# Nine of eleven feed-forward chunks by seven products, on weight pages grown in place by accumulating loads

## The chip, the core and the metric

The kernel runs on one core of one Trainium2 chip. The metric is device time in microseconds of one execution. The weights are float32 in HBM and are streamed through the chip in every execution.

## What is computed

One layer of a hybrid encoder on a sequence of 256 positions with 2048 channels. Two SwiGLU feed-forward layers (5632 hidden channels) stand around a mixer of mLSTM and attention:

```
def _swiglu(x, w1, w3, w2):
    return (jax.nn.silu(x @ w1) * (x @ w3)) @ w2

x   = _layer_norm(ALPHA * x + 0.5 * _swiglu(x, ffn1_w1[i], ffn1_w3[i], ffn1_w2[i]), ln1_g[i], ln1_b[i])
mix = _hybrid_mixer(x, ...)
x   = _layer_norm(ALPHA * x + mix, ln2_g[i], ln2_b[i])
x   = _layer_norm(ALPHA * x + 0.5 * _swiglu(x, ffn2_w1[i], ffn2_w3[i], ffn2_w2[i]), ln3_g[i], ln3_b[i])
x   = x + jax.nn.sigmoid(x @ w_ple_gate[i]) * (p[i] @ w_ple_proj[i])
```

The change touches the two feed-forward layers alone.

## The kernel before

**Matmuls in three parts.** TensorE works here on float32r operands. To keep precision each operand is split into a high part (a cast on ScalarE) and a low part (a subtraction on VectorE), and a product is high x high + high x low + low x high. Weights come as pages: a page is 256 rows by 512 columns of a weight (512 KB, tile `raw`, 128 partitions x 1024 values). `split_one` makes of it two pages `split`: ScalarE's cast at L972, VectorE's subtraction at L976. A *unit* is one page against one half of the sequence (128 positions): six matmuls of 512 columns, lines L1021 to L1023, into a bank `mm` of PSUM. In plain code (`group`) one split page serves two units, one for each half of the sequence.

**Chunks.** The 5632 hidden channels are worked in eleven chunks of 512 columns. A plain chunk has 16 units for the gate (w1), 16 for the hidden part (w3), then evictions, transposes (L247) and the down projection (w2), 16 units a chunk.

**Seven products.** Gate and hidden columns of both halves of the sequence together are a 2 x 2 block product: the activations' halves of the sequence by two halves of the channels, the weights' two halves of the channels by w1 and w3. `seven` does it with seven products instead of eight (numbered m = 1 to 7), four units each, 28 units for a chunk instead of 32. Three products take a page of the weights as it is (b11, b21 of w1, b12, b22 of w3), the others sums: b11 + b12, b11 + b12 + b22, b12 + b22, and the last one plus b21. They also need sums of activations (`forms`), made once for a layer by `form_turn`. Each side page is split for one unit only, where a plain page serves two. Before the change 7 of 11 chunks go this way.

Before, the page b11 + b12 is made at load time: SP loads b12 (L945) and POOL adds b11 to it with an accumulating load (L949, `accum_op=ALU.add`). The other sums are made by VectorE on pages (L308), or, in every second step, by one more accumulating load. The seven results are kept in seven banks, and VectorE adds them up (L404, L413, L452).

**Order.** The order is written out by hand. TensorE, VectorE, ScalarE, POOL and SP each work their instructions off in the order in which the program recorded them. `program` is the list of units in TensorE's order: plain units (`main`), with the side units of the seven-product chunks woven between them evenly (`weave`). `splits_due` records splits ahead of TensorE, up to SPLIT_FFN = 7 split weights at a time; `loads` records loads ahead of the splits, up to RAW_FFN pages. All pages come from one pool of 44 (PAGES). Short pieces of work (evictions, transposes) are recorded by `Sched` when they fall due by a clock that counts TensorE's units; its delays set only the order. Banks of PSUM: eight, in one rotating pool.

## Time and profile before

| what | value |
|---|---|
| time, median of 3 runs | 2230.02 us (2229.87 to 2230.93) |
| span of the profiled execution | 2228.3 us |
| mean granted TensorE clock | 0.998 |
| TensorE, VectorE, ScalarE busy | 99%, 76%, 54% of the span |
| HBM read | 533.56 MB, 240 GB/s over the span |
| plain loads of feed-forward weights (SP) | 639 of 512 KB, median 6.2 us to landing |
| accumulating loads (POOL) | 84 of 512 KB, median 9.0 us to landing |

The first feed-forward layer takes about the first 700 us of the span, the mixer the next 700, the second feed-forward layer about 1430 to 2110 us. In a window's row the columns are the window and its length, then for PE, PEld, DVE, ACT and POOL the busy us and in brackets the number of instructions, then the granted clock, the DMA engines' mean share, and GB/s. In a group's row stand the line, engine and operation, what is written from what, the count, busy us and the mean ns of one, and the idle time before them with what ended it. A busy matmul row is longer than its step to the next, since matmuls are pipelined; the step is read from a timeline.

### The profile page before, as it was taken

Reading aid. Unit: us, or ns where it says so; the run is one execution under the profiler, and the core shown is the slowest. Engines: PE = TensorE matmul, PEld = TensorE weight load, DVE = VectorE, ACT = ScalarE, POOL = GpSimd, SP = SyncE. Lnnn points to the kernel's source line nnn. Section 1 sums busy time; section 2 is a strip of 40 time slices with the busy share of each in tenths; the row PEclk is TensorE's granted clock in tenths of the full one; section 3 lists DMA queues with packets and bytes.
Section 4 is the critical chain, followed back from the end, with each engine's and each line's share of the span. In section 5 each row is a group of like instructions: output and inputs, shape, how many; then the busy total and the mean of one; then the engine's idle time right before and its main releaser. Section 6 shows DMA issues by size and latency. Waiting matters only on the chain.

```text
span 2228.3 us, 27828 instructions
## 1 busy us (share of the span) xinstructions
PE 2209.5 (99%) x10107; PEld 1832.6 (82%) x10107; DVE 1703.1 (76%) x1878; ACT 1197.9 (54%) x1383; POOL 152.3 (7%) x131
## 2 busy tenths in 40 slices
PE   9999999999999999999999999999999999999999
PEld 7888888888887888888888888788888888888878
DVE  6999888989888674654445466798888898989873
ACT  6655655555562655545643354465555555556452
POOL 2100100001000000101100000200100100100000
PEclk9999999999999999999999999999999999999999
DMA  9998999899993755555455566589999989999543
GB/s 333 280 293 278 277 290 305 273 290 288 288 319 97 225 182 169 185 166 169 153 191 193 183 228 216 187 242 295 273 282 289 286 276 299 283 294 321 201 159 96
DMA packets 281354, 537.50 MB, mean 241 GB/s; under 512 B 16832, under 2 KB 25856, under 8 KB 281216
## 3 DMA queue, kind: packets, MB, share of 16 engines
q1 hardware_dynamic: 258368, 491.68, 65.4%
q0 software_dynamic: 22848, 44.05, 11.4%
q8 instruction: 79, 1.29, 0.2%
q14 instruction: 59, 0.48, 0.1%
HBM read 533.56 MB, written 2.10 MB: 240 GB/s over the span
## 4 chain that ended last, share of the span: by engine, by line
PE 96%; DVE 3%; issue 0%; ACT 0%; DMA 0%; DVEq 0%
PE mm L1023 31%; PE mm L1021 31%; PE mm L1022 31%; PE ms L247 1%; DVE xres L368 1%; DVE xres L366 0%; DVE xres L369 0%; DVE stats L353 0%; DVE actT L254 0%; DVE split L976 0%; PE ms L741 0%; PE ms L764 0%; PE ms L692 0%; PE ms L704 0%; PE ms L754 0%
## 5 line engine op out<-in xcount | busy, mean ns | idle before, releaser
L976 DVE TENSOR_TENSOR split<-raw,split 128x1024 fp32r<-128x1024 f32 (+1 forms) x989 | 1162.3, 1206 | 314.5 <-ACT split L972 276.8
L972 ACT CAST split<-raw 128x1024 fp32r<-128x1024 f32 (+1 forms) x989 | 994.8, 1039 | 522.9 <-PE mm L1023 222.0
L1021 PE MATMUL mm<-split,actT 128*128 128x512 f32 (+2 forms) x3168 | 1233.9, 389 | 0.0
L1023 PE MATMUL mm<-split,actT 128*128 128x512 f32 (+2 forms) x3168 | 1223.4, 386 | 8.6 <-DVE actT L254 8.6
L1022 PE MATMUL mm<-split,actT 128*128 128x512 f32 (+2 forms) x3168 | 1221.8, 386 | 0.3 <-DVE split L976 0.3
L1023 PEld LDWEIGHTS mm<-split,actT 128*128 128x128 f32 x3168 | 596.4, 188 | 131.4 <-DVE actT L254 11.6
L1022 PEld LDWEIGHTS mm<-split,actT 128*128 128x128 f32 x3168 | 596.9, 188 | 116.4 <-DVE split L976 0.8
L1021 PEld LDWEIGHTS mm<-split,actT 128*128 128x128 f32 x3168 | 596.9, 188 | 116.3 <-issue 1.0
L949 POOL DMA_DIRECT2D raw<-in_ffn_w_dram x84 | 101.2, 1205 | 1087.4 <-DMA raw<-in_ffn_w_dram 371.6
L308 DVE TENSOR_TENSOR raw<-raw 128x1024 f32<-128x1024 f32 x140 | 170.9, 1221 | 1.0
L249 ACT CAST actT<-ms 128x512 fp32r<-128x512 f32 x84 | 49.1, 589 | 132.6 <-PE ms L247 122.5
L466 DVE SCALAR_TENSOR_TENSOR xres<-mm,xres 128x512 f32<-128x512 f32 x128 | 87.3, 686 | 12.7 <-PE mm L1023 12.5
L413 DVE TENSOR_TENSOR temp<-mm,temp 128x512 f32<-128x512 f32 x98 | 67.4, 687 | 13.1 <-PE mm L1023 11.5
L254 DVE TENSOR_TENSOR actT<-ms,actT 128x512 fp32r<-128x512 f32 x84 | 57.3, 686 | 22.7 <-ACT big L253 11.2
L383 POOL TENSOR_SCALAR xres<-xres 128x512 f32<-128x512 f32 x16 | 26.7, 1675 | 331.5 <-DVE xres L366 300.5
L219 ACT ACTIVATE temp<-mm 128x512 f32<-128x512 f32 (+1 forms) x26 | 14.7, 567 | 53.1 <-PE mm L1023 53.1
L219 ACT ACTIVATE temp<-temp 128x512 f32<-128x512 f32 (+1 forms) x44 | 26.0, 590 | 29.7 <-DVE temp L756 21.9
L219 ACT ACTIVATE big<-mm 128x512 f32<-128x512 f32 x20 | 12.0, 599 | 55.4 <-PE mm L1023 55.4
L215 ACT ACT_TABLE_LOAD x29 | 37.2, 1283 | 0.5
L811 DVE TENSOR_TENSOR big<-mm,big 128x512 f32<-128x512 f32 x16 | 11.1, 692 | 30.0 <-PE mm L1023 30.0
L897 DVE TENSOR_TENSOR temp<-temp,big 128x512 f32<-128x512 f32 (+1 forms) x10 | 5.8, 585 | 36.4 <-ACT temp L219 36.4
L219 ACT ACTIVATE rstd<-mv,eps 128x1 f32<-128x1 f32 x6 | 1.8, 296 | 51.8 <-DVE mv L359 51.8
(113 smaller groups left out, 513.7 us busy)
## 6 DMA issues: line engine op xcount, KB each, us to landing
raw<-in_ffn_w_dram SPq DMA_DIRECT2D x639, 512.0 KB, 6.2
raw<-in_w_in_dram SPq DMA_DIRECT2D x168, 512.0 KB, 3.7
raw<-in_ffn_w_dram POOLq DMA_DIRECT2D x84, 512.0 KB, 9.0
raw<-in_w_out_dram SPq DMA_DIRECT2D x32, 512.0 KB, 4.5
raw<-in_w_ple_gate_dram SPq DMA_DIRECT2D x24, 512.0 KB, 4.9
raw<-in_w_up_m_dram SPq DMA_DIRECT2D x16, 512.0 KB, 3.6
raw<-in_w_up_sb_dram SPq DMA_DIRECT2D x16, 512.0 KB, 4.1
raw<-in_w_ple_gate_dram SPq DMA_DIRECT2D x16, 256.0 KB, 5.2
```

The source lines that it names most:

```text
L219: nc.scalar.activation(out, in_, func, **kw)
L249: nc.scalar.copy(dst[:, 0], ps[:])
L254: nc.vector.tensor_tensor(out=dst[:, 1], in0=ps[:], in1=dst[:, 0], op=ALU.subtract)
L308: nc.vector.tensor_tensor(out=out.tile[:, :, :cols], in0=a.tile[:, :, :cols], in1=b.tile[:, :, :cols], op=ALU.add)
L413: nc.vector.tensor_tensor(out=out, in0=a, in1=b, op=op)
L466: nc.vector.scalar_tensor_tensor(out=xs, in0=ps, scalar=0.5, in1=xs, op0=ALU.mult, op1=ALU.add)
L949: nc.gpsimd.dma_start(out=r.tile[:, :, :r.cols], in_=r.plus, accum_op=ALU.add)
L972: nc.scalar.copy(hi[:, ks], r[:, ks])
L976: nc.vector.tensor_tensor(out=lo[:, ks], in0=r[:, ks], in1=hi[:, ks], op=ALU.subtract)
L1021: nc.tensor.matmul(ps, hi, w[0][:, k, :u.cols], start=first, stop=False)
L1022: nc.tensor.matmul(ps, hi, w[1][:, k, :u.cols], start=False, stop=False)
L1023: nc.tensor.matmul(ps, lo, w[0][:, k, :u.cols], start=False, stop=last)
```

## The change

Nine of eleven chunks go by seven products; chunks 0 and 5 stay plain. `seven` now loads b11 into a page, splits it for product 1, lets POOL add b12 to the same page, splits it for product 5, lets POOL add b22, splits it for product 6, lets VectorE add b21, and splits it for product 4. All of 1 (four units), then all of 5, two empty places in the weave, all of 6, then 2 and 4 in turn, then 7 and 3 in turn. b12 + b22 is always made by VectorE. Results are summed in PSUM: products 1 and 2 in one bank (X), 5 and 4 in one (E), 6 and 3 in one (B), 7 in one (W). B and W are two banks set aside; VectorE writes X - E into B before product 6, ScalarE copies B into W after it, and matmuls accumulate on top. Eight matmuls of ones at the start, in place of five, set these banks up for that. Six banks rotate instead of eight. Up to 12 raw pages may be loaded, if a count of pages in use lets them.

```diff
-RAW_FFN, RAW_MIX, RAW_EDGE = 9, 5, 4
+RAW_FFN, RAW_MIX, RAW_EDGE = 12, 5, 4
-PSUM_BUFS = 8
+PSUM_BUFS = 6
...
+    seeded = [seed_pool.tile([P, COL], F32, name=f"seeded{k}") for k in range(2)]
...
     def seven(wa, wb, rows, col0, cols, act, done):
         n = rows // (4 * P)
-        accs = {m: {} for m in range(1, 8)}
+        banks = {k: {} for k in "XEBW"}
...
+        def grow(raw, src):
+            def load():
+                nc.gpsimd.dma_start(out=raw.tile[:, :, :cols], in_=src.src, accum_op=ALU.add)
+            return load
...
-        units = []
-        for m, sub in ((1, 0), (2, 2)):
-            for i in range(n):
-                units.append(unit(m, i, plain(rows_of(wa, (4 * i + sub) * P, col0, cols)), act, 0, sub))
         for i in range(n):
-            b11, b12, b22, b21 = (rows_of(w, (4 * i + sub) * P, col0, cols)
-                                  for w, sub in ((wa, 0), (wb, 0), (wb, 2), (wa, 2)))
-            t1 = Raw(b12.src, cols, b11.src)
-            t3, add = (Raw(b12.src, cols, b22.src), None) if i % 2 else (b12, plus(b12, b12, b22))
-            first = Weight(t1, [t1], [])
-            units += [
-                unit(5, i, first, act.forms, 0, 0),
-                unit(7, i, Weight(t3, [t3, b22], [t3], add), act.forms, 1, 0),
-                unit(6, i, Weight(t1, [], [], plus(t1, t1, b22), first), act.forms, 0, 2),
-                unit(4, i, Weight(b21, [b21], [t1, b21], plus(b21, t1, b21)), act, 1, 2),
-                unit(3, i, Weight(b22, [], [b22]), act.forms, 1, 2),
-            ]
-        return units
+            t, b21 = quarter(wa, i, 0), quarter(wa, i, 2)
+            w1, w5, w6 = Weight(t, [t], []), Weight(t, [], []), Weight(t, [], [])
+            w1.then, w5.then = grow(t, quarter(wb, i, 0)), grow(t, quarter(wb, i, 2))
+            one.append(unit(1, i, w1, act, 0, 0, "X", True))
+            five.append(unit(5, i, w5, act.forms, 0, 0, "E", True))
+            six.append(unit(6, i, w6, act.forms, 0, 2, "B", False))
+            two.append(unit(2, i, Weight(b21, [b21], []), act, 0, 2, "X", False))
+            four.append(unit(4, i, Weight(t, [], [t, b21], plus(t, b21)), act, 1, 2, "E", False))
+            b12, b22 = quarter(wb, i, 0), quarter(wb, i, 2)
+            rest.append(unit(7, i, Weight(b12, [b12, b22], [b12], plus(b12, b22)), act.forms, 1, 0, "W", False))
+            rest.append(unit(3, i, Weight(b22, [], [b22]), act.forms, 1, 2, "B", False))
+        lead = two[:1]
+        for i in range(n):
+            lead += two[i + 1:i + 2] + four[i:i + 1]
+        return one + five + [None, None] + six + lead + rest
...
+            def done(m, banks):
+                ps = {k: v["ps"][:] for k, v in banks.items() if v}
+                if m == 5:
+                    e = temp()
+                    nc.scalar.copy(e[:], ps["E"])
+                    banks["B"]["ps"], banks["W"]["ps"] = seeded
+                    both(banks["B"]["ps"][:], ps["X"], e[:], ALU.subtract)
+                    drop()
+                elif m == 6:
+                    nc.scalar.copy(banks["W"]["ps"][:], ps["B"])
...
-        gate, hidden = zip(*(up(c) for c in (0, 3, 6, 9)))
+        gate, hidden = zip(*(up(c) for c in (0, 5)))
...
-        main = flat(hidden[0] + gate[1] + down(0) + hidden[1] + down(1) + gate[2] + down(2, 3)
-                    + hidden[2] + down(4) + gate[3] + down(5, 6) + hidden[3] + down(7) + rest[:8])
-        program.extend(main[:8] + weave(main[8:], [u for c in (1, 2, 4, 5, 7, 8, 10) for u in up7(c)]))
+        main = flat(hidden[0] + gate[1] + down(0) + down(1) + down(2) + down(3) + down(4) + hidden[1] + down(6) + down(5, 7))
+        program.extend(main[:8] + weave(main[8:] + flat(rest[:8]), [u for c in (1, 2, 3, 4, 6, 7, 8, 9, 10) for u in up7(c)]))
...
-    warm(WARM)
+    for ps in seeded:
+        for k in range(4):
+            nc.tensor.matmul(ps[:, k * P:(k + 1) * P], ones[:], ones[:], start=k == 0, stop=k == 3)
...
-        while pos["load"] < most and pos["raw"] < (4 if pos["at"] < 6 else limits(pos["split"])[0]):
+        while (pos["load"] < most and pos["raw"] < (4 if pos["at"] < 6 else limits(pos["split"])[0])
+               and (mixing() or pages[0] + pos["raw"] + 2 * limits(pos["split"])[1] < PAGES)):
...
+        if w.then:
+            w.then()
```

Where the instructions stand. POOL's queue before, for the second seven-product chunk of the first layer (each row is one accumulating load, named by the page it adds to; the page was loaded by SP ahead of it):

```order
L949 DMA raw_1211<-in_ffn1_w1_dram 128x2x512
L949 DMA raw_1325<-in_ffn1_w1_dram 128x2x512
L949 DMA raw_1372<-in_ffn1_w3_dram 128x2x512
L949 DMA raw_1478<-in_ffn1_w1_dram 128x2x512
L949 DMA raw_1598<-in_ffn1_w1_dram 128x2x512
L949 DMA raw_1618<-in_ffn1_w3_dram 128x2x512
```

Each page is added to once. The same queue now, for the third chunk by seven products:

```order
L328 DMA raw_1414<-in_ffn1_w3_dram 128x2x512
L328 DMA raw_1427<-in_ffn1_w3_dram 128x2x512
L328 DMA raw_1460<-in_ffn1_w3_dram 128x2x512
L328 DMA raw_1474<-in_ffn1_w3_dram 128x2x512
L328 DMA raw_1414<-in_ffn1_w3_dram 128x2x512
L328 DMA raw_1427<-in_ffn1_w3_dram 128x2x512
L328 DMA raw_1460<-in_ffn1_w3_dram 128x2x512
L328 DMA raw_1474<-in_ffn1_w3_dram 128x2x512
```

Eight instead of six a chunk, four pages twice each, and each stands behind a split that reads the page.

ScalarE's queue before, in the first such chunk, around a page that an accumulating load made (raw_875, then the same page with more added; the rows between are plain pages):

```order
L972 CAST split_1023<-raw_875 128x1024
L972 CAST split_1034<-raw_888 128x1024
L972 CAST split_1047<-raw_918 128x1024
L972 CAST split_1066<-raw_875 128x1024
L972 CAST split_1078<-raw_960 128x1024
```

The page is split for product 5 and again, after VectorE has added b22 to it, for product 6. ScalarE's queue now, in the third chunk, from the last cast for product 5 to the copy of bank E (mm_1722 is E):

```order
L995 CAST split_1685<-raw_1474 128x1024
L995 CAST split_1696<-raw_1501 128x1024
L266 CAST actT_1714<-ms_1709 128x512
L995 CAST split_1718<-raw_1414 128x1024
L995 CAST split_1729<-raw_1520 128x1024
L995 CAST split_1746<-raw_1427 128x1024
L995 CAST split_1756<-raw_1460 128x1024
L995 CAST split_1767<-raw_1474 128x1024
L443 COPY temp_1777<-mm_1722 128x512
```

The copy stands behind the casts of all four pages for product 6. VectorE's queue at the same place, to the seed of bank B (seeded0; mm_1635 is X):

```order
L999 TENSOR_TENSOR split_1719<-raw_1414,split_1718 128x1024
L999 TENSOR_TENSOR split_1730<-raw_1520,split_1729 128x1024
L999 TENSOR_TENSOR split_1747<-raw_1427,split_1746 128x1024
L999 TENSOR_TENSOR split_1757<-raw_1460,split_1756 128x1024
L999 TENSOR_TENSOR split_1768<-raw_1474,split_1767 128x1024
L437 TENSOR_TENSOR seeded0_78<-mm_1635,temp_1777 128x512
```

The seed stands behind the four splits for product 6; before the change no matmul waited for an eviction of its own chunk.

More of the change, by code (lines that the diff above doesn't have):

```diff
@@ L134, in __init__ @@
         self.start, self.stop, self.done = start, stop, done
+        self.onto = False
         tile.uses += 1
+        act.planned(chunk, tt)
 class Boundary:
@@ L153, in weave @@
             while at < len(side) and at * n < seen * len(side):
-                out.append(side[at])
+                if side[at] is not None:
+                    out.append(side[at])
                 at += 1
@@ L300, in seven, with unit @@
         n = rows // (4 * P)
-        accs = {m: {} for m in range(1, 8)}
-        def unit(m, i, tile, src, half, sub):
-            return Unit(tile, half, accs[m], src, i, sub, i == 0, i == n - 1, lambda ps, t, m=m: done(m, ps))
-        def plus(out, a, b):
+        banks = {k: {} for k in "XEBW"}
+        def unit(m, i, tile, src, half, sub, bank, first):
+            u = Unit(tile, half, banks[bank], src, i, sub, first and i == 0, i == n - 1,
+                     lambda ps, t, m=m: done(m, banks))
+            u.onto = not first
+            return u
@@ L1027 @@
             splits.pop(j)
+        if u.act.used(u.chunk, u.tt):
+            pages[0] -= 1
         if u.stop:
```

90 lines of the change are left out of this document (46 added, 44 removed).

## The prediction

> **What bounds the kernel now.** I read the page's first and fourth parts, the busy time of a long stretch inside the first feed-forward layer, and the list of waits there, in that order. A window's columns are: length; PE, PEld, DVE, ACT, POOL busy (instructions); granted clock; DMA share; GB/s.
>
> ```profile
> PE 2209.5 (99%) x10107; PEld 1832.6 (82%) x10107; DVE 1703.1 (76%) x1878; ACT 1197.9 (54%) x1383; POOL 152.3 (7%) x131
> PE 96%; DVE 3%; issue 0%; ACT 0%; DMA 0%; DVEq 0%
> 60.00:640.00 580.00, 580.00 (x2599) 480.47 (x2598) 517.52 (x513) 336.91 (x351) 49.30 (x41) 1.00 0.94 287
> ACT split L972 <- DMA raw<-in_ffn_w_dram: 8.8, 6, 2.4
> ```
>
> The chain that ended last is 96% TensorE, and in the feed-forward stretch TensorE never idles at full clock. But VectorE is busy 517.52 / 580 = 89% there and the DMA engines 94%. So matmuls taken out are gained only as long as the two nearly full resources deliver on time. Now they do: ScalarE waited 8.8 us in 580 for a weight page.
>
> What a matmul costs, and what a stall of TensorE does besides its own length, stands around the first layer norm:
>
> ```profile
> 704.15 0.39 PE L1023 MATMUL mm<-split,actT 128*128 128x512 f32 x1
> ...
> 704.83 0.39 PE L1023 MATMUL mm<-split,actT 128*128 128x512 f32 x1
> ...
> 706.06 0.40 PE L1022 MATMUL mm<-split,actT 128*128 128x512 f32 x1
> 709.16 0.50 PE L1023 MATMUL mm<-split,actT 128*128 128x512 f32 x1 [2.71 <-DVE actT L254]
> ...
> 710.78 0.63 PE L1022 MATMUL mm<-split,actT 128*128 128x512 f32 x1
> 711.21 0.63 PE L1023 MATMUL mm<-split,actT 128*128 128x512 f32 x1
> 710.00:720.00 10.00, 9.59 (x42) 7.55 (x41) 9.33 (x17) 1.96 (x4) 0.00 (x0) 0.83 0.09 27
> ```
>
> Three steps in 0.68 us: a matmul takes 0.227 us, a unit of six 1.36 us. After 2.71 us of idling the step is 0.43 us for a while and the granted clock of the next 10 us is 0.83, so 1.7 us more are lost.
>
> The accumulating loads, which the change leans on, are priced by these rows (queue q0 is POOL's, q1 is SP's):
>
> ```profile
> q1 hardware_dynamic: 258368, 491.68, 65.4%
> q0 software_dynamic: 22848, 44.05, 11.4%
> raw<-in_ffn_w_dram SPq DMA_DIRECT2D x639, 512.0 KB, 6.2
> raw<-in_ffn_w_dram POOLq DMA_DIRECT2D x84, 512.0 KB, 9.0
> DMA to landing us min/median/max: 5.7/9.0/12.8
> ```
>
> q0: 11.4% of 2228.3 us is 254 us on each of the 16 engines, 3.02 us for each of 84 loads. q1: 65.4% is 1457 us for 491.68 MB, or 938 loads of 512 KB: 1.55 us each. An accumulating load thus holds all 16 engines twice as long as a plain one. The quickest landed after 5.7 us, so about 2.7 us are fixed.
>
> **The change part by part.** Prices of one instruction:
>
> ```profile
> L976 DVE TENSOR_TENSOR split<-raw,split 128x1024 fp32r<-128x1024 f32 x955 | 1139.7, 1224 | 299.3 <-ACT split L972 263.9 <-PE mm L1022 16.8 <-issue 5.4
> L972 ACT CAST split<-raw 128x1024 fp32r<-128x1024 f32 x955 | 975.7, 1054 | 516.4 <-PE mm L1023 222.0 <-PE mm L1022 181.6 <-DVE raw L308 38.5
> L308 DVE TENSOR_TENSOR raw<-raw 128x1024 f32<-128x1024 f32 x140 | 170.9, 1221 | 1.0
> L413 DVE TENSOR_TENSOR temp<-mm,temp 128x512 f32<-128x512 f32 x98 | 67.4, 687 | 13.1 <-PE mm L1023 11.5
> L419 ACT COPY temp<-mm 128x512 f32<-128x512 f32 x14 | 8.3, 590 | 30.4 <-PE mm L1023 30.4
> ```
>
> *Two more chunks by seven products.* A chunk of 32 units becomes one of 28. Two chunks in each of two layers: 4 x 4 x 6 = 96 matmuls less, 96 x 0.227 = **-21.8 us**, all on TensorE, which is the path.
>
> *VectorE.* Per layer the splits go from 16 x 4 + 28 x 7 + 88 = 348 to 16 x 2 + 28 x 9 + 88 = 372, +24 x 1.22 = +29.4 us; page sums from 70 to 72, +2.4 us; evictions of up-projections from 9 x 7 + 2 x 4 = 71 to 4 x 9 + 2 x 2 = 40, -31 x 0.69 = -21.3 us. Net +10.5 us on some 0.89 x 650 = 580 us, over 640 us: 92%. It stays below TensorE, so I cost it at nothing; its cover is the 8% that are left. ScalarE gains 24 casts (25 us) and two copies a chunk, from 58% to about 63%: hidden.
>
> *DMA volume.* Plain loads per layer fall from 320 to 264, accumulating ones rise from 42 to 72: 320 x 1.55 + 42 x 3.02 = 623 us against 264 x 1.55 + 72 x 3.02 = 627 us. The mean load is unchanged. What changes is when it comes.
>
> *Accumulating loads move from the prefetch into the chunk.* This is the term that decides. Before, such a load was issued with the prefetch, several splits ahead of its use. Now the page is split for product 1, b12 is added, it is split for product 5, b22 is added, and it is split for product 6. POOL issues four, then four again, and the second four stand behind splits that wait for the first four. Then comes the seed: bank B = X - E. ScalarE's copy of E and VectorE's subtraction stand behind the casts and splits for product 6 on their in-order queues, behind all four of them in 8 chunks of 18, behind three in 10. And the first matmul of product 6 accumulates onto bank B, so TensorE, in order, stands still with all woven plain work behind it until seven or eight accumulating loads have landed.
>
> What that needs, worked out from the rows: one split (1.05 + 1.22 = 2.3 us), the fixed 2.7 us, eight times 3.02 = 24.2 us of all 16 engines, then a cast, a split and the seed, 1.05 + 1.22 + 0.69 = 3.0 us (the copy, 0.59 us, lies beside the split). That is 32.2 us, or 29.2 us where seven suffice. What covers it is TensorE's work between the matmul whose end lets the first split run and product 6. Counted from the program's semaphores: in the sixteen regular chunks 119 to 134 matmuls with their transposes, on average 28.8 us at 0.227 us each; in the first chunk of layer 1 31.3 us, in that of layer 2 37 us. So the need is above the cover even if no plain load shares the engines, by 3.4 and 0.4 us.
>
> Plain loads do share them. In this stretch side pages are held, not freed, so only woven plain weights let new loads through: 28.8 us hold 21 units, 184 of 436 of them plain, about 9 units or 4.5 loads. I take four, 6.2 us. The waits are then 9.6 us (eight chunks) and 6.6 us (eight), 4.1 us in layer 1's first and none in layer 2's first: 76.8 + 52.8 + 4.1 = **+133.7 us**. The bounds: without plain loads 8 x 3.4 + 8 x 0.4 = 30 us. At most I let a load take 5.05 us, from the longest landing, (12.8 - 2.7) / 2, if that one had stood behind another: 8 + 8 x 5.05 = 48.4 and 43.4 us, waits of 19.6 and 14.6 us, 273.6 us. I take the value nearest the mean packet time of q0, since q0 will be the fuller queue there.
>
> *The clock.* Seventeen waits longer than the 2.71 us above, at 1.7 us each: **+28.9 us**. Nothing at least, if the cases above are the short ones.
>
> *Small edits, together.* The seeded banks are set up by eight matmuls of ones instead of five:
>
> ```profile
> 1.12 2.50 PE L914 MATMUL ms<-ones 128*128 128x128 f32 x10 [1.12 <-DVE eps L228]
> 4.34 0.87 PE L247 MATMUL ms<-ident,xres 128*128 128x128 f32 x3 [0.72 <-DMA xres<-in_x_dram]
> ```
>
> Sixteen records of 0.25 us end at 5.1 us, not 3.6, where x lets TensorE go on at 4.34: +0.8 us. Six rotating banks instead of eight: X and E hold two, the plain pair two, two are free; the old scheme held up to five of eight for a chunk, so nothing. Deeper raw limit with a page count: nothing to a few us, inside the plain loads' term.
>
> *Sum.* 2228.3 - 21.8 + 0.8 + 133.7 + 28.9 = 2369.9 us. The profiled span is 1.7 us below the median of the runs shown, 2230.02 us, so I predict **2372 us**.
>
> A rule that speaks for the opposite, on its own: the Trainium skill, DMA: Bandwidth & Descriptors, section on the anatomy of one DMA on the SWDGE path, gives a fixed 2.0 us plus bytes / 436 GB/s. By it 512 KB move in 1.2 us (an estimate from that page), eight in 9.6 us, and the chain would be hidden. The rows show 3.02 us for this accumulating form, so I do not follow it.
>
> **The rivals.**
> *The growth is hidden (faster).* It decides at 8.0 + 8 x s = 28.8 us, s = 2.6 us per accumulating load, with plain loads yielding. Then only the removed matmuls count: 2230.0 - 21.8 + 0.8 = 2209 us. For it: 3.02 us includes sharing. Against it: no sum of rows reaches 2.6, and plain loads come on top.
> *Growth alone counts (slightly slower).* Plain loads run before or after it: 30 us of waits, half of them (8 x 1.7) with a lowered clock: 2230.0 - 21.8 + 0.8 + 30.4 + 13.6 = 2253 us.
> *Growth at 5.05 us a load (much slower).* 2230.0 - 21.8 + 0.8 + 273.6 + 12.1 + 28.9 = 2524 us, with 43.4 - 31.3 = 12.1 us for layer 1's first chunk. The median landing of 9.0 us speaks for crowding, the lower plain traffic in the stretch against it.
> *DMA volume is the bound.* The share is 94% now and the volume is unchanged: the old pace holds and the time stays at 2230 us. Against it: ScalarE waits 8.8 us in all for DMA now.
>
> **How the numbers follow.** Forecast 0.57 (its own range 2300 to 2440 us), hidden 0.12, growth alone 0.15, 5.05 us a load 0.12, volume 0.04. The low end of the range, 2240 us, leaves out the hidden and the volume case; the high end, 2490 us, takes in most of what lies between the forecast and the third rival. No change can be told within 0.2%, 4.5 us: faster 0.12, same 0.04, slower 0.84.
>
> **What would show it.** Right: TensorE's share falls to about 93%, and the largest wait of TensorE is that of the first seeded matmul for VectorE's seed (L437), some 16 times 6 to 10 us. ScalarE's split waits for DMA in the hundreds of us. POOL's loads land after a median above 12 us. The granted clock falls below 1.0 seventeen times more. VectorE's share does not rise above 90% of the layer. Wrong: no such wait, accumulating loads landing in 6 to 9 us though issued four in a row. The weakest step is the cover of 28.8 us: were VectorE to run the first split earlier, or the four plain loads be gone by then, each microsecond a chunk is 18 us in the sum.

## The result, and the profile after

The kernel after takes 2355.45 us (median of 4 runs, 2350.49 to 2361.89) against 2230.11 us before (4 runs, 2229.87 to 2230.93): a ratio of 1.0565, with a 95% interval of 1.0546 to 1.0584. It is slower by 125 us. The profiled execution took 2361.89 us with a span of 2360.2 us, 6 us above the median.

The page of the kernel after, its first, third and last parts (busy time; DMA queues with packets, MB and share of 16 engines' span; DMA issues with KB each and median us to landing):

```profile
PE 2236.6 (95%) x10017; PEld 1839.7 (78%) x10017; DVE 1734.9 (74%) x1884; ACT 1260.3 (53%) x1471; POOL 221.4 (9%) x191
...
q1 hardware_dynamic: 227904, 432.95, 55.8%
q0 software_dynamic: 39168, 75.51, 18.0%
...
raw<-in_ffn_w_dram SPq DMA_DIRECT2D x527, 512.0 KB, 6.2
...
raw<-in_ffn_w_dram POOLq DMA_DIRECT2D x144, 512.0 KB, 9.6
```

There are 90 matmul records fewer (96 taken out, six more in the set-up), and yet TensorE's busy time rose and its share fell. The same long stretch of the first layer, with the columns of the prediction's window:

```profile
60.00:640.00 580.00, 536.38 (x2318) 438.17 (x2317) 489.41 (x479) 335.61 (x362) 69.42 (x58) 0.96 0.84 237
```

TensorE issues 2318 matmuls in these 580 us where it issued 2599, at a granted clock of 0.96 instead of 1.00. VectorE is less busy than before (489 against 518 us) and the DMA engines too (0.84 against 0.94). So nothing is full any more; something waits. What TensorE waited for (us in total, times, longest), and after it ScalarE's largest wait:

```profile
PE seeded L1046 <- DVE seeded L437: 84.2, 16, 8.9
PE mm L1046 <- ACT actT L258: 12.8, 4, 6.7
PE mm L1048 <- DVE actT L272: 7.5, 6, 2.7
PE mm L1047 <- DVE split L999: 4.7, 8, 0.8
...
ACT split L995 <- DMA raw<-in_ffn_w_dram: 250.2, 132, 7.3
```

The first line is new: in 16 of 18 chunks the first matmul of product 6 waits 5.3 us on average for VectorE's seed of bank B. All lines of TensorE's waits come to 118.3 us, 13.8 us before. One such wait in order of time, in the fifth chunk: POOL's accumulating loads, ScalarE, VectorE and TensorE (start, length, then what the engine idled for just before).

```profile
348.50 1.20 POOL L328 DMA_DIRECT2D raw<-in_ffn_w_dram  x1 [50.16 <-DVE split L999]
...
369.33 1.20 POOL L328 DMA_DIRECT2D raw<-in_ffn_w_dram  x1 [2.35 <-DVE split L999]
```

```profile
373.74 1.05 ACT L995 CAST split<-raw 128x1024 fp32r<-128x1024 f32 x1 [2.54 <-DMA raw<-in_ffn_w_dram]
376.26 1.99 ACT L995 CAST split<-raw 128x1024 fp32r<-128x1024 f32 x2 [1.48 <-DMA raw<-in_ffn_w_dram]
378.16 0.58 ACT L443 COPY temp<-mm 128x512 f32<-128x512 f32 x1
```

```profile
377.34 2.36 DVE L999 TENSOR_TENSOR split<-raw,split 128x1024 fp32r<-128x1024 f32 x2 [1.29 <-ACT split L995]
379.62 0.68 DVE L483 SCALAR_TENSOR_TENSOR xres<-mm,xres 128x512 f32<-128x512 f32 x1
380.22 0.69 DVE L437 TENSOR_TENSOR seeded<-mm,temp 128x512 f32<-128x512 f32 x1
```

```profile
374.48 0.40 PE L1048 MATMUL mm<-split,actT 128*128 128x512 f32 x1
380.96 0.80 PE L1046 MATMUL seeded<-split,actT 128*128 128x512 f32 x1 [6.09 <-DVE seeded L437]
381.56 0.63 PE L1047 MATMUL seeded<-split,actT 128*128 128x512 f32 x1
381.99 0.63 PE L1048 MATMUL seeded<-split,actT 128*128 128x512 f32 x1
```

Eight loads are issued from 348.5 to 369.3. The casts start as their pages land, 2.5 to 3.7 us apart. TensorE had finished product 5 and all plain work ahead of product 6 at 374.7, but ScalarE's copy of E (L443) runs only behind three of the casts for product 6, at 378.2, and the seed behind VectorE's splits, at 380.2. The fourth cast stands behind the copy, so this seed needed seven of the eight loads. When TensorE goes on at 380.96 its steps are 0.43 us instead of 0.227. The granted clock around this wait, by windows (the column behind the engines' busy times):

```profile
371.40:374.80 3.40, 3.40 (x18) 2.55 (x16) 1.09 (x1) 1.05 (x1) 0.00 (x0) 1.00 1.13 225
374.80:378.40 3.60, 0.08 (x1) 0.00 (x0) 2.29 (x2) 2.13 (x3) 0.00 (x0) 1.00 1.10 242
378.40:381.00 2.60, 0.04 (x1) 0.04 (x1) 2.51 (x4) 1.41 (x3) 0.00 (x0) 0.50 0.30 97
381.00:385.20 4.20, 4.20 (x10) 3.34 (x11) 4.19 (x5) 2.45 (x3) 0.00 (x0) 0.50 0.02 4
385.20:388.60 3.40, 3.40 (x16) 2.81 (x16) 3.05 (x4) 2.00 (x2) 0.00 (x0) 0.99 0.46 131
```

The clock is halved 3.7 us after TensorE fell idle and stays so for 6.8 us, of which 4.2 us are work: some 2 us lost. The Trainium skill, TensorE: Matmul & The Clock Gate, part 1, says that half rate comes after at least one idle window of about 3.4 us; this wait agrees, but a step of 2.92 us between two matmuls (at 450 us) was also followed by a half-speed stretch, of 3.41 us. The windows also show that the DMA engines are full until the last accumulating load lands and idle right after it (1.10, then 0.30 and 0.02): SP's next plain load waited 12.7 us, until 385.8, for a matmul (L1048) that runs behind the start of product 6.

Put together against the span before (+131.9 us): matmuls -21.8, set-up +0.35 (the row of the first transpose moved from 4.34 to 4.69), waits 118.3 - 13.8 = +104.5, and what is left, +48.9 us, is the clock and gaps too short for the list of waits. Of it, matmul steps over 0.3 us inside the half-speed stretches, summed over the trace's rows, make 43.2 - 4.3 = 38.9 us.

### The profile page after: what moved, and what is told of

Its sections match the earlier page's. It is cut to its first block, busy times and chain, and to the rows that moved or that the text cites. A ratio compares the mean times of both kernels' runs of the same rounds, so it can differ in the third digit from the quotient of the medians.

```text
span 2360.2 us, 27588 instructions
## 1 busy us (share of the span) xinstructions
PE 2236.6 (95%) x10017; PEld 1839.7 (78%) x10017; DVE 1734.9 (74%) x1884; ACT 1260.3 (53%) x1471; POOL 221.4 (9%) x191
## 3 DMA queue, kind: packets, MB, share of 16 engines
q0 software_dynamic: 39168, 75.51, 18.0%
## 5 line engine op out<-in xcount | busy, mean ns | idle before, releaser
L999 DVE TENSOR_TENSOR split<-raw,split 128x1024 fp32r<-128x1024 f32 (+1 forms) x1037 | 1219.1, 1207 | 429.4 <-ACT split L995 406.7
L995 ACT CAST split<-raw 128x1024 fp32r<-128x1024 f32 (+1 forms) x1037 | 1042.2, 1037 | 659.2 <-DMA raw<-in_ffn_w_dram 250.2
L1046 PE MATMUL mm<-split,actT 128*128 128x512 f32 (+2 forms) x2704 | 1060.3, 392 | 15.2 <-ACT actT L258 12.8
L1048 PE MATMUL mm<-split,actT 128*128 128x512 f32 (+2 forms) x2704 | 1047.8, 387 | 8.8 <-DVE actT L272 7.5
L1047 PE MATMUL mm<-split,actT 128*128 128x512 f32 (+2 forms) x2704 | 1047.3, 387 | 4.7 <-DVE split L999 4.7
L1046 PEld LDWEIGHTS mm<-split,actT 128*128 128x128 f32 x2704 | 513.1, 190 | 118.7 <-ACT actT L258 15.0
L1048 PEld LDWEIGHTS mm<-split,actT 128*128 128x128 f32 x2704 | 512.4, 190 | 116.4 <-DVE actT L272 10.1
L1047 PEld LDWEIGHTS mm<-split,actT 128*128 128x128 f32 x2704 | 513.4, 190 | 106.0 <-DVE split L999 7.6
L328 POOL DMA_DIRECT2D raw<-in_ffn_w_dram x144 | 173.9, 1217 | 1105.4 <-DMA raw<-in_ffn_w_dram 589.7
L1046 PE MATMUL seeded<-split,actT 128*128 128x512 f32 x432 | 180.6, 418 | 84.2 <-DVE seeded L437 84.2
L1047 PE MATMUL seeded<-split,actT 128*128 128x512 f32 x432 | 177.6, 411 | 0.0
L1048 PE MATMUL seeded<-split,actT 128*128 128x512 f32 x432 | 176.6, 409 | 0.0
L1046 PEld LDWEIGHTS seeded<-split,actT 128*128 128x128 f32 x432 | 86.5, 200 | 109.0 <-DVE seeded L437 91.0
L483 DVE SCALAR_TENSOR_TENSOR xres<-mm,xres 128x512 f32<-128x512 f32 x144 | 98.3, 685 | 7.0 <-PE mm L1048 7.0
L1048 PEld LDWEIGHTS seeded<-split,actT 128*128 128x128 f32 x432 | 86.9, 201 | 19.3
L1047 PEld LDWEIGHTS seeded<-split,actT 128*128 128x128 f32 x432 | 87.0, 201 | 17.8
L266 ACT CAST actT<-ms 128x512 fp32r<-128x512 f32 x84 | 48.9, 587 | 81.8 <-PE ms L264 79.3
L272 DVE TENSOR_TENSOR actT<-ms,actT 128x512 fp32r<-128x512 f32 x84 | 57.2, 685 | 22.2 <-ACT big L271 10.8
L236 ACT ACTIVATE temp<-mm 128x512 f32<-128x512 f32 (+1 forms) x36 | 20.5, 570 | 44.9 <-PE mm L1048 44.9
```

The source lines that it names most:

```text
L236: nc.scalar.activation(out, in_, func, **kw)
L266: nc.scalar.copy(dst[:, 0], ps[:])
L272: nc.vector.tensor_tensor(out=dst[:, 1], in0=ps[:], in1=dst[:, 0], op=ALU.subtract)
L328: nc.gpsimd.dma_start(out=raw.tile[:, :, :cols], in_=src.src, accum_op=ALU.add)
L483: nc.vector.scalar_tensor_tensor(out=xs, in0=ps, scalar=0.5, in1=xs, op0=ALU.mult, op1=ALU.add)
L995: nc.scalar.copy(hi[:, ks], r[:, ks])
```

## The experiments

All ratios are to the kernel before, run on the same chip. The last two columns are worked out from the matmul rows of each trace alike: what the steps over 0.6 us from one matmul to the next have above 0.227 us (gaps), and what shorter steps inside half-speed stretches have above it (clock). Comments in the code are notes for the reader.

| kernel | median us | ratio, 95% interval | waits for the seed us | gaps us | clock us |
|---|---|---|---|---|---|
| before | 2230 | 1 | none | 14.8 | 4.3 |
| after | 2355.45 | 1.0565, 1.0546 to 1.0584 | 84.2 | 124.9 | 43.2 |
| e1_half_growth | 2288.99 | 1.0263, 1.0248 to 1.0279 | 35.4 | 70.0 | 24.0 |
| e2_no_seed | 2304.21 | 1.0333, 1.0317 to 1.0348 | no seed | 84.0 | 21.3 |
| e3_seed_first | 2273.91 | 1.0195, 1.0180 to 1.0210 | 2.6 | 61.5 | 11.9 |
| e4_vector_adds | 2370.04 | 1.0623, 1.0606 to 1.0641 | 86.3 | 130.6 | 48.9 |
| e5_filler | 2380.62 | 1.0676, 1.0657 to 1.0696 | 6.7 | 73.1 | 9.9 |
| e6_new_seven | 2241.40 | 1.0049, 1.0032 to 1.0066 | none | 21.9 | 8.3 |
| e7_first_spread | 2263.01 | 1.0146, 1.0131 to 1.0162 | none | 50.3 | 9.8 |
| e8_first_two_adds | 2277.37 | 1.0210, 1.0193 to 1.0227 | 10.8 | 61.3 | 14.2 |
| e9_filler_bank | 2352.57 | 1.0552, 1.0536 to 1.0568 | 33.6 | 72.1 | 21.0 |
| e10_plain_growth | 2217.91 | 0.9947, 0.9933 to 0.9961 | none | 21.8 | 5.5 |
| e11_first_spread_eight | 2222.43 | 0.9968, 0.9956 to 0.9981 | none | 16.4 | 5.3 |
| e12_old_scheme_nine | 2239.06 | 1.0041, 1.0027 to 1.0055 | no seed | 36.3 | 10.8 |

**e1: half of the second growth.**

```
-        def grow(raw, src):
+        def grow(raw, src, first):
             def load():
-                nc.gpsimd.dma_start(out=raw.tile[:, :, :cols], in_=src.src, accum_op=ALU.add)
+                n = cols if first else cols // 2
+                nc.gpsimd.dma_start(out=raw.tile[:, :, :n], in_=src.src[:, :, :n], accum_op=ALU.add)
...
```

> The second accumulating load of each page adds 256 of the 512 columns of b22, so products 6 and 4 leave out half of b22; every instruction, wait and queue place stays. Theory (the seed's wait is the run of eight accumulating loads, about 2.95 us each, that the splits ahead of the seed wait for): a chunk's loads take 4 x 2.95 + 4 x 1.5 = 17.8 us instead of 23.6, so the 5 to 6 us waits vanish in most chunks; TensorE's wait for the seed falls from 84 us to under 25, the half-speed stretches between layer norms from seventeen to under six, time 2215 to 2260 us. Rival 1 (the cost is in VectorE's and ScalarE's own work, or in six PSUM banks instead of eight): nothing changes, 2340 to 2365 us. Rival 2 (a packet of 1 KB holds a DMA engine as long as one of 2 KB): also nothing, and the DMA rows tell it from rival 1.

Measured: 2289 us. A quarter of the accumulated bytes less took 66 us off and more than half of the waits for the seed, so the loads matter and rival 1 falls. The size was missed: 29 us above the theory's range, 35.4 us of waits instead of under 25, and eleven half-speed stretches between the layer norms instead of under six. In the page, q0's share fell less than the bytes would have it:

```profile
q0 software_dynamic: 39168, 56.63, 14.9%
```

14.9% of 2287.2 us over 144 loads is 2.37 us of packet time on each engine for one; with 2.95 us for the full ones (18.0% of 2360.2 us over 144 in the kernel after) the half ones took 1.78 us. Rival 2 is true in a small part: half the bytes are 60% of the time.

**e2: no seed.**

```
-            six.append(unit(6, i, w6, act.forms, 0, 2, "B", False))
+            six.append(unit(6, i, w6, act.forms, 0, 2, "B", True))
...
-                    both(banks["B"]["ps"][:], ps["X"], e[:], ALU.subtract)
...
-        if u.start:
+        if u.start and not u.acc.get("ps"):
```

> Product 6 starts its bank afresh: VectorE's subtraction X - E is gone, so the outputs lack that sum; all loads, splits and products stay. Theory (TensorE waits because the seed stands behind the splits of the grown pages in VectorE's queue): product 6 now needs only its own first page, the fifth of the eight accumulating loads instead of the eighth, some 10 us earlier; the wait falls to under 15 us, the clock stays at full speed but for the layer norms, time 2205 to 2235 us. Rival (the accumulating loads are late for TensorE itself, wherever the seed stands): the wait moves to product 6's second to fourth page (TensorE on split), 40 to 80 us of it, 2290 to 2350 us.

Measured: 2304 us, 69 us above the theory's range and inside the rival's, but not for the rival's reason: the wait for the seed is gone, and it did not move to product 6's pages (split waits of product 6 are 2.7 us). What TensorE waits for now:

```profile
PE mm L1045 <- DVE xres L482: 15.8, 8, 4.8
PE mm L1045 <- ACT actT L258: 12.6, 4, 7.6
PE mm L1045 <- ACT actT L266: 12.2, 2, 6.2
PE mm L1047 <- DVE actT L272: 9.4, 9, 2.7
```

These are down sums that free a PSUM bank (xres) and turned hidden chunks (actT): other results that also stand behind the splits on the two in-order queues. One of the two waits for L266, of 6 us, in ScalarE's rows:

```profile
366.63 1.04 ACT L994 CAST split<-raw 128x1024 fp32r<-128x1024 f32 x1 [1.39 <-DMA raw<-in_ffn_w_dram]
367.58 0.58 ACT L266 CAST actT<-ms 128x512 fp32r<-128x512 f32 x1
```

So the seed is only the first victim. While a cast waits for an accumulating load, everything behind it on ScalarE and VectorE waits too.

**e3: the seed ahead of the splits.**

```
+            w6.hold = gate if i >= HOLD else None      # HOLD = 1; gate opens when product 5 is done
...
         while pos["split"] < most and len(splits) < limits(pos["split"])[1]:
+            if weights[pos["split"]].hold and weights[pos["split"]].hold[0]:
+                break
```

> The splits of product 6's second to fourth page are put into the queues of ScalarE and VectorE only after the seed of their chunk; nothing else changes, and the loads are as slow as before. Theory (the seed's place behind these splits is the wait, since product 6 needs its second page only 2.7 us after its first): in the fifth chunk product 6 could start at 374.7 and needs its pages at 374.7, 377.4, 380.1 and 382.8, while they land at 370.1, 373.7, 376.2 and 379.9 and are split some 2 us later, so nothing waits; waits for the seed under 25 us, time 2210 to 2245 us. Rival 1 (the loads themselves are too slow for product 6): the wait turns into TensorE on split, 40 us or more, 2290 to 2350 us. Rival 2 (the splits held back are then late for the pages that follow): TensorE waits for split 1 to 3 us a chunk, 2245 to 2290 us.

Measured: 2274 us. The place in the queue was the wait for the seed:

```profile
PE seeded L1052 <- DVE seeded L441: 2.6, 4, 0.8
```

84.2 us became 2.6 us with loads as slow as before (9.5 us from issue to landing, 2.95 us of packet time). That 81 us of 125 went by order alone is the clearest finding. But the time is 29 us over the upper bound. It lies in rival 2's range, yet rival 2 does not name the rest: TensorE's waits for splits come to 9.4 us in the whole run, not 1 to 3 us a chunk. One wait of the fifth chunk, in ScalarE's and then in TensorE's rows:

```profile
354.94 1.04 ACT L999 CAST split<-raw 128x1024 fp32r<-128x1024 f32 x1 [1.88 <-DMA raw<-in_ffn_w_dram]
355.89 0.58 ACT L268 CAST actT<-ms 128x512 fp32r<-128x512 f32 x1
```

```profile
356.52 0.80 PE L1052 MATMUL mm<-split,actT 128*128 128x512 f32 x1 [5.87 <-ACT actT L268]
```

ScalarE waits for the eighth load, and the cast of a turned chunk (L268), for which TensorE has been waiting, stands behind it: the mechanism of e2, with another victim.

**e4: VectorE makes the second growth.**

```
+            if i in BY_VECTOR:                          # (0, 1, 2, 3)
+                extra = quarter(wb, i, 2)
+                w5.then, w6 = None, Weight(t, [extra], [extra], plus(t, extra), w5)
```

> All four second growths of a chunk are made by VectorE: b22 comes by a plain load on SP's queue into a page of its own and is added to t by a tensor_tensor; the first four accumulating loads (b12) stay, and the bytes loaded stay. Theory (eight accumulating loads in series on one queue are the wait): four take 12 us, well inside the cover of 25 to 29 us; waits for the seed under 15 us; VectorE gains 72 adds of 1.14 us, 82 us in all, and in the layers it goes from 84% to some 91% busy, which it was before; time 2205 to 2240 us. Rival 1 (VectorE is already the bound in the chunks): each add shows, up to 82 us minus what the waits give back, 2300 to 2360 us. Rival 2 (the plain loads of b22 push back the loads that follow on SP's queue): ScalarE waits longer for raw pages and TensorE for split, 2250 to 2300 us.

Measured: 2370 us, a clear miss: only four accumulating loads a chunk, and the waits for the seed are what they were. VectorE's rows of the fifth chunk (L334 is the add, L441 the seed):

```profile
367.02 1.23 DVE L1003 TENSOR_TENSOR split<-raw,split 128x1024 fp32r<-128x1024 f32 x1 [1.27 <-ACT split L999]
...
369.89 1.22 DVE L334 TENSOR_TENSOR raw<-raw 128x1024 f32<-128x1024 f32 x1
371.03 1.22 DVE L1003 TENSOR_TENSOR split<-raw,split 128x1024 fp32r<-128x1024 f32 x1
...
379.04 1.22 DVE L334 TENSOR_TENSOR raw<-raw 128x1024 f32<-128x1024 f32 x1
380.18 2.35 DVE L1003 TENSOR_TENSOR split<-raw,split 128x1024 fp32r<-128x1024 f32 x2
382.45 0.68 DVE L487 SCALAR_TENSOR_TENSOR xres<-mm,xres 128x512 f32<-128x512 f32 x1
383.05 0.69 DVE L441 TENSOR_TENSOR seeded<-mm,temp 128x512 f32<-128x512 f32 x1
```

From 367.0 us to the seed VectorE has no gap. The splits for product 6 still stand ahead of the seed and now bring an add each, 16 us of queue in a row. The time is 10 us above rival 1's range too. My theory that the number of accumulating loads alone is the wait falls; it is whatever the work ahead of the seed needs, be it loads or VectorE's own time.

**e5: TensorE kept busy during the wait.**

```
+        if u.filler:                                    # product 6's first unit, 22
+            warm(u.filler)
```

> 22 matmuls of ones (128x128, 0.23 us each, 5.0 us in all) into a bank that nobody reads stand ahead of product 6's first matmul in each chunk, so TensorE works through most of the wait for the seed; the wait itself stays. Theory (the half-speed stretches follow from TensorE's idle stretch): most idle stretches become shorter than 2.9 us, the half-speed stretches go from 20 to under eight, and the 39 us by which matmuls in them are longer fall to under 15; in the four chunks that waited under 3.4 us the filler costs 2 to 3 us each, 10 us together; time 2325 to 2340 us. Rival (the clock falls for another reason, such as what the chunk's matmuls draw): stretches and time stay, 2350 to 2370 us.

Measured: 2380.6 us, slower than both said. The filler cost more than planned, and its bank came free late:

```profile
L933 PE MATMUL ms<-ones 128*128 128x128 f32 x796 | 103.1, 294 | 25.9 <-DVE xres L486 25.9
```

103 us of filler ran, where 90 were planned, in eight chunks behind a wait of its own. What can be kept is the clock: matmuls in half-speed stretches lost 9.9 us, not 43.2, in ten such stretches instead of twenty (under eight were forecast).

**e9: the filler in a free bank.**

```
+        for _ in range(u.filler):                       # 16
+            nc.tensor.matmul(seeded[1][:, 0:P], ones[:], ones[:], start=False, stop=False, skip_group_check=True)
```

> As e5_filler, mended: there the filler's scratch bank was released late by VectorE, so the filler ran behind the wait in part (25.9 us of waits at its own line, 103 us of filler in all). Now 16 matmuls of ones (0.26 us each, 4.2 us a chunk, 75 us in all) go into the bank that the chunk's later copy overwrites, free for some 40 us by then. In twelve of the eighteen chunks they fit into the wait, in four by 2 to 3 us, in two there is none: 16 us are added, the rest is free. Theory (half speed follows from TensorE's idle stretch): matmuls in half-speed stretches lose under 15 us instead of 43, so 2335 to 2350 us. Rival (half speed has another cause): 2365 to 2380 us.

Measured: 2352.6 us, 3 us below the kernel after with overlapping intervals, and just above the theory's range. The filler's 67 us took 50.6 us out of the waits for the seed (84.2 to 33.6), and the clock term fell by 22 us, from 43.2 to 21.0, not below 15. Half speed does follow TensorE's idling; the filler that overran the shorter waits ate most of what that gave.

**e6: the new scheme with seven chunks.**

```
-        gate, hidden = zip(*(up(c) for c in (0, 5)))
+        gate, hidden = zip(*(up(c) for c in (0, 3, 6, 9)))
...
+        program.extend(main[:8] + weave(main[8:], [u for c in (1, 2, 4, 5, 7, 8, 10) for u in up7(c)]))
```

> The scheme of the kernel after with the seven chunks and the order of the kernel before: 14 chunks grow their pages instead of 18, and each stands beside more of the ordinary products, so that by the order written down some 38 us of TensorE's work lie between a chunk's first accumulating load and product 6, instead of 28.5 (counted alike for both). The matmuls are as many as before. Theory (a run of 29 to 32 us of loads against the cover): the run fits, waits for the seed fall under 20 us, time 2230 to 2260 us. Rival 1 (each chunk of the new scheme costs its 8 us whatever stands around it): 14 x 8.3 = 116 us, 2340 us. Rival 2 (six PSUM banks, or the queues' order in general, cost something by themselves): little wait for the seed but over 2260 us.

Measured: 2241.4 us, as the theory had it, and rival 1's 2340 us is far off. In the trace 35.5 us of TensorE's work lie on average between a chunk's first accumulating load and product 6, instead of 26.9 (the first chunk of each layer left out), and no seed is late, although the runs of loads, 31.5 to 34.6 us, are no shorter. The scheme itself, with its loads, seeds and six rotating banks, costs at most the 10 us by which this is above the kernel before, and rival 2 too is out as a main cause.

**e7 and e8: more cover, or fewer accumulating loads, on top of e3.**

```
-        return one + five + [None, None] + six + lead + rest
+        early = [v for u in one + five for v in (u, None, None)]
+        return early + [None, None] + six + lead + rest
```

> As e3_seed_first, and two more units of ordinary products stand behind every unit of products 1 and 5, which gives a chunk's eight accumulating loads some 5 us more of cover (33.8 instead of 28.5 us by the order). The rest of the chunk is packed closer. Theory (what e3_seed_first has left, some 47 us of gaps in TensorE beyond those of the kernel before, are results that stand behind splits in ScalarE's and VectorE's queues, and these splits wait for the accumulating loads): with more cover the splits wait less, 2235 to 2260 us. Rival (what is left comes from elsewhere: the six banks, the closer order): 2265 to 2290 us.

> As e3_seed_first, and the last two of the eight growths of a chunk are made by VectorE from a plain load, as in e4_vector_adds: six accumulating loads, 18 us instead of 24, and 36 adds of 1.14 us, 41 us more for VectorE. Theory (the same as for e7_first_spread): ScalarE waits less for accumulating loads, 2235 to 2260 us. Rival (VectorE's queue is what is left): the adds and the splits behind them delay the sums that release PSUM banks, 2275 to 2320 us.

Measured: e7 2263.0 us, 3 us over its range; e8, with BY_VECTOR = (2, 3), 2277.4 us, in its rival's range and no gain over e3's 2273.9. More cover helped by 11 us and took gaps from 61.5 to 50.3 us. In e8 VectorE was busy 522 us of the 580 us stretch instead of e3's 506, and 10.8 us of waits for the seed came back, so fewer loads were paid for by more work on the other queue. Nine chunks keep some 35 us of gaps in e7 beyond the 14.8 us of the kernel before, in 51 steps over 0.6 us instead of 11, most of them up to 2.2 us long and spread over many lines; I did not find one cause for them.

**e10: the same loads without the addition.**

```
-                nc.gpsimd.dma_start(out=raw.tile[:, :, :cols], in_=src.src, accum_op=ALU.add)
+                nc.gpsimd.dma_start(out=raw.tile[:, :, :cols], in_=src.src)
```

> The eight growths of a chunk are plain loads on the same queue, at the same places, of the same bytes: they overwrite the page instead of adding to it, so the sums of two quarters are left out. Theory (the accumulation makes a load hold the DMA engines for 3 us instead of 1.55, and eight of these in series are the wait): q0's packets take 144 x 1.6 = 230 us an engine instead of 425, the run of eight shrinks from 29 to some 17 to 20 us, waits for the seed under 20 us, time 2215 to 2250 us. Rival (the queue's own latency, 9.6 us from issue to landing, and the order on it are the wait, accumulating or not): landing stays over 8 us, waits over 50 us, 2310 to 2360 us.

Measured: 2217.9 us, as the theory had it. Bytes, issues, queue and order are those of the kernel after; the page's q0 and landing rows, and the window of the first layer:

```profile
q0 software_dynamic: 20736, 75.51, 9.8%
...
raw<-in_ffn_w_dram POOLq DMA_DIRECT2D x144, 512.0 KB, 5.7
```

```profile
60.00:640.00 580.00, 576.19 (x2566) 475.77 (x2565) 532.97 (x521) 369.98 (x398) 46.33 (x64) 0.99 0.78 264
```

A load's packets take 9.8% of 2216.3 us / 144 = 1.51 us on each engine instead of 2.95, it lands in 5.7 us instead of 9.6, and no wait for a seed is left. VectorE at 92% of the stretch costs little: gaps are 7 us above those of the kernel before. The issue on POOL is shorter too, as the rows of L328 show (fastest, median and slowest in ns), in the kernel after and in e10:

```profile
L328 POOL DMA_DIRECT2D raw<-in_ffn_w_dram x144: 1194/1203/1712, 41.6 to 2139.6; - x144
L328 POOL DMA_DIRECT2D raw<-in_ffn_w_dram x144: 722/724/915, 41.6 to 2003.9; - x144
```

Eight times 0.48 us are 3.8 us at most. The run of the fifth chunk, from the first issue to the last landing, went from 31.4 to 21.1 us, so the issue is not the main part. This is the test that settles the cause: of the 146 us that the kernel after is above what the removed matmuls would give (2209 us), 137.5 us go when the loads do not accumulate.

**e12: the count alone, by the old scheme.** The kernel before, with the chunks and the order of the kernel after:

```
+        gate, hidden = zip(*(up(c) for c in (0, 5)))
+        program.extend(main[:8] + weave(main[8:] + flat(rest[:8]), [u for c in (1, 2, 3, 4, 6, 7, 8, 9, 10) for u in up7(c)]))
```

> The count alone: the scheme of the kernel before (sums by VectorE, eight PSUM banks, no accumulating growth) with nine of eleven chunks in the order of the kernel after. 96 matmuls fewer than before, 21.8 us. Theory (in a chunk of the old scheme VectorE has more work than TensorE leaves it time for; by the counts of its instructions it would be busy 98% of the layer): TensorE waits for VectorE in many small steps, 2225 to 2290 us. Rival (the count alone pays): 2206 to 2215 us, and then the new scheme was not needed.

Measured: 2239.1 us, slower than before by 0.4%. Its window of the first layer:

```profile
60.00:640.00 580.00, 571.32 (x2537) 470.62 (x2537) 565.29 (x570) 350.30 (x371) 61.34 (x51) 0.99 1.00 307
```

VectorE is busy 565 / 580 = 97% and the DMA engines are full; this run does not separate the two, though of TensorE's 34 us of waits 26 are for VectorE. The old scheme does not return the removed matmuls either, but it loses 30 us against their 2209 us, the new one 146.

**e11: a version that beats both.** e7 with eight chunks, 0, 4 and 8 ordinary:

```
-        gate, hidden = zip(*(up(c) for c in (0, 5)))
+        gate, hidden = zip(*(up(c) for c in (0, 4, 8)))
```

> As e7_first_spread with eight seven-product chunks of eleven (chunks 0, 4 and 8 ordinary): 48 matmuls more than e7 (10.9 us), and a ninth less of everything that waits. Theory (what is lost grows as the chunks come closer: 11 us with seven spread over the layer, 50 us with nine): the gaps beyond those of the kernel before fall from 35 to 15 us, 2238 to 2252 us, so it does not beat the kernel before. Rival (the first spread and the seed's place leave no loss at this density): 2225 to 2235 us, at or below the kernel before.

Measured: 2222.43 us, 0.3% faster than the kernel before (ratio 0.9956 to 0.9981), which my theory had ruled out; the time is just below the rival's range. Its page (busy time) and the window:

```profile
PE 2199.3 (99%) x10065; PEld 1824.0 (82%) x10065; DVE 1680.1 (76%) x1840; ACT 1223.8 (55%) x1441; POOL 202.0 (9%) x175
```

```profile
60.00:640.00 580.00, 580.00 (x2599) 480.34 (x2598) 507.27 (x497) 350.25 (x381) 68.87 (x58) 1.00 0.90 260
```

TensorE does not idle in the stretch and keeps its clock. 48 matmuls fewer than before are 10.9 us; 7.4 us of them arrive (2229.79 us before, on that chip). Losses do not grow evenly with the count: between eight and nine chunks gaps go from 16 to 50 us.

## Why the prediction was right, and where its sizes were off

2372 us were predicted and 2355.45 measured, and the mechanism is the one that the largest term described: product 6's first matmul waits for a seed that stands behind splits, which wait for accumulating loads. e3 and e10 show both halves of that separately. Term by term:

- *Matmuls, -21.8 us.* Not visible by itself. e11 returns 7.4 of 10.9 us for half the cut, and 2.6 of the missing 3.5 us stand in its gaps and its clock term, so the price of a matmul held.
- *The seed's waits, +133.7 us: measured 84.2.* The term was too large by 49.5 us, and the step that failed in it is "eight times 3.02". 3.02 us is packet time, and packets overlap on the engines, so it is longer than the pace. In the seventh chunk, where one plain load was issued during the run and the DMA share from 505 to 520 us is 1.11, the casts started 2.54 us apart as pages landed:

```profile
508.24 1.05 ACT L995 CAST split<-raw 128x1024 fp32r<-128x1024 f32 x1 [0.96 <-DMA raw<-in_ffn_w_dram]
510.78 1.05 ACT L995 CAST split<-raw 128x1024 fp32r<-128x1024 f32 x1 [1.49 <-DMA raw<-in_ffn_w_dram]
```

  In that run the packets of a load still sum to 2.98 us an engine, so it is not sharing with plain loads that makes 3.02 out of 2.54. The run took 26.1 us from first issue to last landing and its wait was a step of 1.9 us; the other run with one plain load issued (the 16th) took 27.5 us, with a step of 3.3 us. With three to five plain loads (twelve of the sixteen regular chunks) runs took 27.7 to 31.7 us, with seven 37 us and steps of 7.8 and 9.2 us.

  The other parts of the term held. The plain loads: while a seed's loads ran, q1 moved the bytes of 2.0 to 7.8 plain loads, 4.7 on average. The cover: TensorE worked 25.2 to 29.6 us from the first issue to product 6, 26.9 on average, and the split ahead of that issue adds 2.3 us, so the 28.8 us that I named the weakest step was right. Estimated with 2.54 us a load, the need is 2.3 + 2.7 + 20.3 + 3.0 = 28.3 us and 4.7 x 1.55 = 7.3 us for plain loads: waits of 6.8 us behind eight loads and of 4.3 us behind seven, half of the regular chunks each, 5.5 us on average, where 5.3 were measured.
- *Chunks without a wait.* The first chunk of layer 2 had none, as forecast. The first of layer 1 was to wait 4.1 us for its seed and did not; TensorE waited there 6.66 and 2.29 us for ScalarE's forms (actT L258), and 2.00 and 1.85 us in layer 2's first. The first form of each pair stood behind such a cast, the second waited for a sum (L283) that stands behind splits on VectorE. The 20 us of waits on other lines (104.5 - 84.2) are what the prediction did not see: results on the two queues are delayed, not the seed alone. e2 and e3 show it.
- *The clock, +28.9 us: measured about 39.* There are seventeen more half-speed stretches, as forecast (from three to twenty, without the one at the end of each run; the first at 64.4 us, 13.65 us long, the last at 2259.2, 3.41 us), but that the count agrees is luck: fifteen follow waits for the seed, two the waits for forms in the first chunks, and the wait of the seventh chunk has none. 1.7 us each was taken from a wait of 2.71 us; after waits of 6 us the stretch lasts 6.8 us, and some 2 us are lost.
- *The total is luck in part.* On the spans 141.6 us more were forecast and 131.9 measured. The seed's waits were 49.5 us too high; the waits on other lines (20.3 us) were left out, and the clock with the short gaps was 20.0 us too low (48.9 against 28.9). These errors go opposite ways, so the total is better than its terms.
- *Set-up, +0.8: measured 0.35.* The sixteen records started at 1.11 us and the next transpose at 4.69, so a record took 0.22 us, not 0.25.
- *VectorE, nothing.* It held, 84% in the stretch; e10 runs at 92% with 7 us more of gaps than the kernel before, e12 at 97% with 21.5 us more.
- *What would show it.* TensorE's share (95% against about 93), the seed as the largest wait (16 times; 5.3 us on average, below the 6 to 10 named) and ScalarE's wait for DMA (250 us) came as described. The landing median did not: 9.6 us, not above 12. A likely reason, not tested alone: the second four loads are held back on POOL's queue until the first have landed and been split (in the fifth chunk POOL idled 2.0 to 3.5 us ahead of each), so part of the crowding passes before the issue.

The rule of the Trainium skill that the prediction set against its own price (DMA: Bandwidth & Descriptors, anatomy of one DMA on the SWDGE path: an estimate of 1.2 us for 512 KB) would have been right about the outcome had the loads been plain: e10 measured 1.51 us of packet time a load, and the growth was hidden. For accumulating loads the trace decides, with 2.95 us of packet time and landings no closer than some 2.5 us.

## What to carry to other kernels

A transfer that delays an instruction on an in-order queue delays everything written behind it there, so ask of a slow load not only who reads it but what stands behind its reader; putting one waited-for result ahead of such readers (e3) was worth 81 us without making any load faster. Count a run of dependent loads against the work of the bounding engine that stands beside it: the same scheme cost 0.5% with 38 us of cover by the program's order and 5.7% with 28.5. When a saving is paid with delays, try the step between: eight chunks kept 7.4 of their 10.9 us, where nine in the same form (e7) ended 32 us above the kernel before.

## What the hardware showed that was not expected

The packets of an accumulating load of 512 KB take 2.95 us on each of the 16 DMA engines, those of a plain one on the same queue, of the same bytes and at the same places, 1.51 us, and it shows 39168 / 144 = 272 packets against 20736 / 144 = 144. Half the columns bring it to 1.78 us, with the same number of packets. Packet time is not yet the pace: with hardly any plain load beside them accumulating loads landed 2.54 us apart, at 2.98 us of packet time each.

In the traces half-speed stretches last 3.41 us or a small multiple of it, and longer ones tend to follow longer waits: in the kernel after, the seed's step of 1.9 us left none, those of 2.9 to 3.3 us one of 3.41 us, those of 5.8 to 6.7 us one of 6.83 us, and the two longest (7.8 and 9.2 us) 10.24 us. It is not a fixed rule: in e2 a step of 4.02 us left none and one of 6.4 us one of 10.24 us, and in e4 two steps of 8.04 us left 6.83 us each.
